# The third inner problem of a fast-product FFN makes its weight sums on VectorE; transposes and a plain weight tile move one or two products later

## The chip, the cores and the metric

The kernel runs on one NeuronCore of a Trainium2 chip. The metric is the device time of one execution, in microseconds (us). Three runs of the kernel before took 1898.81, 1896.77 and 1898.53 us, median 1898.53. TensorE is written PE here, VectorE DVE, ScalarE ACT, GpSimd POOL and SyncE SP, as the profile has them.

## The reference

Two layers, each a gated mixer of three branches and then a SwiGLU FFN, with a DeepNorm residual around both. x has 512 rows and 1024 columns, everything is float32. The change touches the FFN alone:

```python
u = jnp.einsum('bsd,df->bsf', x, w_ffn_in[l])
u_gate, u_up = jnp.split(u, 2, axis=-1)
ffn = jnp.einsum('bsf,fd->bsd', jax.nn.silu(u_gate) * u_up, w_ffn_out[l])
x = _layer_norm(DEEPNORM_ALPHA * x + ffn, ln2_g[l], ln2_b[l])
```

The hidden width is 2816 for the gate and for the up half each, that is 22 tiles of 128 columns.

## The kernel before

**Float32 by three products.** Each operand is carried as a high part and a low part. ACT casts the high part and DVE subtracts to get the low part (for weights: class `Staged`, lines 259 and 260, tiles `wh` and `wl`, read from a staging tile `st`). `mm3` (lines 122 to 124) then issues three matmuls for one product of tiles: high by high, high by low, low by high. Where activations are the stationary operand (`product`, output tile `pf`) the second of the three, line 123, already needs `wl`; where weights are stationary (`proj_T`, output `pt`) only the third does.

**Inner problems with seven products.** Columns 0 to 2047 of gate and up are made as four "inner problems" p, q, r, u (`u_fin(0..3, ...)`), of 512 gate and 512 up columns each. One splits into two by two blocks and is made with seven block products instead of eight (m1, m2, y, v, x, g, h). A product is one item: 2 row blocks of 4 times 3 matmuls of 128x512, 24 in all. Its weights are a quadrant of the matrix or a sum of quadrants; quadrant (i, j) means row half i, and gate (j = 0) or up (j = 1). Two classes make these sums:

- `Chain` keeps one staging tile `a` and adds quadrants to it by accumulating DMAs from POOL's queue (line 178): m1 uses (0,0); y uses (0,0)+(0,1), then v and m2 load fresh quadrants, and x and h use `a` after a second and a third accumulation. With the pair of transfers for g ("c") that is four loads on SP and four accumulations on POOL.
- `Close` loads `a` = (0,0)+(0,1) early (a load and one accumulation, "ahead_a"), loads (0,0) again for m1, (1,1) for v and (1,0) for m2, and lets DVE make the sums for x and h: `d += a` at v (line 233) and `e += d` at m2 (line 239). With "c" that is five loads on SP, two accumulations on POOL, and two additions of 128x2048 on DVE.

Before the change p and r are `Chain`, q and u are `Close`. The output product of the FFN has two problems of the same kind, o and w, both `Chain`; the six hidden tiles 16 to 21 are plain (`u_ffn(i)`, 48 matmuls each), the last two of them, 20 and 21, between products of o and w.

**What follows a product.** The gate half of a problem goes through tanh on ACT (line 1201), two DVE operations (1202 and, with the up half, 1210), and so into `nat`. `s_turn(pb, hf)` then transposes two such row tiles on PE (line 1222, eight 128x128 transposes, output `ph`), and ACT copies the two banks out (line 1224, `hf`). `s_ready`, `s_differ`, `s_sums` and `s_rest` make the operands of o and w from these.

**What sets the order.** A list of items, written out by hand (lines 1364 to 1377), gives the order of the products; the groups behind an item are pieces of work done between its row blocks. `run_items` fetches weights ahead until three weight tiles are in hand: three buffers for `wh` and `wl` rotate, so the split of an item's weights can begin when the item three before it has left PE. There are four staging tiles (`NSTAGE`), and a load can be issued on SP only when the tile's last reader is done. All loads stand in SP's queue in one order, the accumulations in POOL's. Each engine takes its instructions strictly in its own order, which a scheduler has fixed when the kernel is built: an instruction that waits holds up all that stands behind it.

Of the kernel before, what the change touches and what calls it, by code (L numbers as in the profile page):

```python
# [56 lines left out]
def trunk(ctx, tc, x_in, xT_in, w_in, ret_norm_g, da_norm_g, lq1, lk1, lq2, lk2, w_a, w_b, w_c, b_merge, w_out,  # L57
# [19 lines left out]
    def g(dt=F32, name="g"):  # L77
        return gp.tile([P, 512], dt, tag="g", name=name)
# [4 lines left out]
    def bank(name="ps"):  # L83
        return psp.tile([P, 512], F32, tag="ps", name=name)
# [256 lines left out]
    def proj_T(act, wt, c0, nk=KT, ps=None, half=None):  # L341

        ps = bank("pt") if ps is None else ps
        sl = slice(0, S) if half is None else slice(256 * half, 256 * half + 256)
        for k in range(nk):
            a = act[k]
            mm3(ps[:, sl], wt.hi[:, k, c0:c0 + P], wt.lo[:, k, c0:c0 + P], a.hi[:, sl], a.lo[:, sl],
                k == 0, k == nk - 1)
        return ps
# [188 lines left out]
    def item(specs, fn, *groups):  # L538

        items.append((specs, fn, groups))  # L540
# [62 lines left out]
    def layer(l):  # L603
# [7 lines left out]
        v = {}  # L611
# [116 lines left out]
        def u_two(hv, acts, left_done, right_done):  # L728

            t, onto = {}, {"x": "m1", "g": "m1", "h": "m1", "v": "y"}  # L730

            def it(name, use):
                def fn(wt):
                    for j in range(2):
                        t[name, j] = ps = product(acts, name, j, wt, t.pop((onto.get(name), j), None))
                        if name in ("x", "g"):
                            t["m1", j] = ps
                        use(j, ps)
                        between()
                return [getattr(hv, name)], fn  # L740

            def copy(to):
                def use(j, ps):
                    t[to, j] = g(name="t" + to)
                    nc.scalar.copy(t[to, j], ps)  # L745
                return use

            def m2(j, ps):
                c = t.pop(("c11", j))
                nc.vector.tensor_add(c, c, ps)  # L750
                left_done(j, c)

            def x(j, ps):
                c = t.pop(("c12", j))
                nc.vector.tensor_sub(c, c, ps)
                right_done(j, c)

            def gg(j, ps):
                c = t.pop(("c22", j))
                nc.vector.tensor_sub(c, c, ps)  # L760
                right_done(2 + j, c)

            def h(j, ps):
                left_done(2 + j, ps)

            use = {"m1": copy("c11"), "m2": m2, "y": copy("c22"), "v": copy("c12"), "x": x, "g": gg, "h": h}
            return {"c": hv.ahead_c, "a": getattr(hv, "ahead_a", None), **{k: it(k, fn) for k, fn in use.items()}}
# [87 lines left out]
        def v_away(dst, wd):  # L855


            def done(t, c):
                for hf in range(2):
                    s = g(F32R, "vhl")  # L860
                    s3 = s.rearrange("p (h x) -> p h x", x=2 * wd)
                    src = c[:, 256 * hf:256 * hf + 256].rearrange("p (h x) -> p h x", x=wd)
                    part_hi(s3[:, :, 0:wd], src)
                    part_lo(s3[:, :, wd:2 * wd], src, s3[:, :, 0:wd])
                    dst[t, hf] = dram.tile([P, 512], F32, name=f"v{l}_{wd}_{t}_{hf}")
                    nc.sync.dma_start(dst[t, hf], f(s))
            return done
# [237 lines left out]
        def u_rvg(hp):  # L1105
            return u_two(Close(W, 0, 4, (RV + 512 * hp, RG + 512 * hp)), xq,
                         functools.partial(rv_done, hp), functools.partial(rg_done, hp))

        w, p, q = u_two(Close(W, 0, 4, (CV, DV)), xq, v_away(cv, 64), v_away(dv, 128)), u_rvg(0), u_rvg(1)
# [73 lines left out]
        def ffn_spec(i):  # L1183
            w = w_ffn_in[l]
            return ([w[:, P * i:P * i + P], w[:, FFN + P * i:FFN + P * i + P]], KT)
# [4 lines left out]
        def ffn_done(i, pg, pu):  # L1190
            t = g(name="fth")
            nc.scalar.activation(t, pg, AF.Tanh, scale=0.5)
            nc.vector.scalar_tensor_tensor(t, t, 1.0, pg, op0=ALU.add, op1=ALU.mult)
            nc.vector.tensor_mul(t, t, pu)
            hid[i] = t
# [17 lines left out]
        def s_turn(pb, hf):  # L1213

            def fn():
                rows = [nat.pop((pb, 2 * hf + j)) for j in range(2)]
                for fp in range(2):
                    ps = bank("ph")
                    for i in range(2):
                        for j in range(2):  # L1220
                            o, c = 256 * i + P * j, P * (2 * fp + i)
                            nc.tensor.transpose(ps[:, o:o + P], rows[j][:, c:c + P], ident)
                    t = half[pb, hf, fp] = g(name="hf")
                    nc.scalar.activation(t, ps, AF.Copy, scale=0.5)
            return fn
# [3 lines left out]
        def s_ready(gi, fp):  # L1229
            def fn():  # L1230
                pa, pc, k = 2 * gi, 2 * gi + 1, 8 * gi + 2 * fp
                tw = twins[gi, fp] = Twins(half.pop((pa, 0, fp)), half.pop((pa, 1, fp)))
                tw.ready(half.pop((pc, 0, fp)))
                hid[k], hid[k + 1] = tw.each
            return fn

        def s_differ(gi, fp):
            def fn():
                twins[gi, fp].difference(half.pop((2 * gi + 1, 1, fp)))
            return fn  # L1240

        def s_sums(gi, fp):
            def fn():
                twins[gi, fp].sums()
            return fn

        def s_rest(gi, fp):
            def fn():
                twins.pop((gi, fp)).rest()
            return fn  # L1250
# [8 lines left out]
        def s_x1(k):  # L1259
            def fn():  # L1260
                if k == 0:
                    x1q.update({i: Quarters(x1T[i], x1T[i + 4]) for i in range(4)})
                x1q[k].sums(x1f.pop(k), x1f.pop(k + 4))
            return fn

        def s_natural(*ts):
            def fn():
                for t in ts:
                    x1["n"].natural(t)
            return fn  # L1270

        def u_fin(pb, kind):

            return u_two(kind(w_ffn_in[l], 0, 4, (512 * pb, FFN + 512 * pb)), x1q,
                         functools.partial(gate_half, pb), functools.partial(gated, pb))
# [13 lines left out]
        def u_ffn(i):  # L1289
            def fn(wt):  # L1290
                pg = proj_T(x1T, wt, 0)
                pu = proj_T(x1T, wt, P)
                ffn_done(i, pg, pu)
            return [ffn_spec(i)], fn
# [64 lines left out]

            return specs, (plain, chase)[hf]  # L1360

        p, q, r, u = u_fin(0, Chain), u_fin(1, Close), u_fin(2, Chain), u_fin(3, Close)
        o, w = fout_items(0), fout_items(1)
        for (specs, fn), *groups in [
            (u_ffn_first([16, 17]), [s_natural(0)], [s_x1(0)]), (p["m1"], [s_x1(1)], [s_x1(2)]),
            (u_ffn(18), [s_x1(3), s_natural(1)], [p["c"]]), (p["m2"], [s_natural(2)], [s_natural(3)]), (p["y"],),
            (p["v"], [q["a"]]), (u_ffn(19),), (p["x"],), (q["m1"],), (p["g"], [s_turn(0, 0)]), (q["y"],), (p["h"],),
            (q["v"], [q["c"]]), (q["m2"], [s_turn(0, 1)]), (q["x"],), (r["m1"],), (q["g"], [s_turn(1, 0)]), (r["m2"], [r["c"]]), (q["h"],),
            (r["y"], [u["a"]]), (r["v"], [s_turn(1, 1)]), (u["m1"],), (r["x"],), (u["y"], [s_ready(0, 0)]), (r["g"], [s_turn(2, 0)]),
            (u["v"], [s_ready(0, 1), u["c"]]), (r["h"],),  # L1370
            (u["m2"],), (o["m1"], [s_turn(2, 1)]), (u["x"], [s_differ(0, 0)], [s_differ(0, 1)]), (o["m2"],),
            (u["g"], [s_turn(3, 0)], [o["c"]]), (o["y"],), (u["h"], [s_sums(0, 0)], [s_sums(0, 1)]),
            (o["v"], [s_rest(0, 0)], [s_rest(0, 1)]), (u_ffn(20), [s_turn(3, 1)]), (o["x"], [s_ready(1, 0)], [s_ready(1, 1)]),
            (w["m1"], [s_differ(1, 0)]), (o["g"], [s_differ(1, 1)], [w["c"]]), (w["m2"], [s_sums(1, 0)]), (o["h"], [s_sums(1, 1)]),
            (w["y"], [s_rest(1, 0)]), (u_ffn(21), [s_rest(1, 1)], [s_hid(16, 17, 18)]), (w["v"], [s_hid(19, 20, 21)]), (w["x"],),
            (fout_rest(0),), (w["g"],), (w["h"],), (fout_rest(1),),
        ]:
            item(specs, fn, *groups)
# [59 lines left out]
```

## Time and profile before

| what | value |
|---|---|
| median of three runs | 1898.53 us |
| the profiled execution | 1898.61 us, of which the span from the first to the last instruction is 1896.8 us |
| PE busy, share of the span | 1870.7 us, 99% |
| DVE busy | 1344.4 us, 71% |
| ACT busy | 973.2 us, 51% |
| mean granted clock of PE | 0.997 |
| transfers | 297.69 MB, mean 157 GB/s |

The spans on PE, DVE and ACT overlap, so their times don't add. The profile's waits say for an idle stretch of an engine which instruction of which other engine ended it. The two FFN stretches that the change touches run from about 679 to 852 us (layer 0) and from about 1622 to 1796 us (layer 1).

### The profile page before, as it was taken

Reading aid. Unit: us, or ns where it says so; the run is one execution under the profiler, and the core shown is the slowest. Engines: PE = TensorE matmul, PEld = TensorE weight load, DVE = VectorE, ACT = ScalarE, POOL = GpSimd, SP = SyncE. Lnnn points to the kernel's source line nnn. Section 1 sums busy time; section 2 is a strip of 40 time slices with the busy share of each in tenths; the row PEclk is TensorE's granted clock in tenths of the full one; section 3 lists DMA queues with packets and bytes.
Section 4 is the critical chain, followed back from the end, with each engine's and each line's share of the span. In section 5 each row is a group of like instructions: output and inputs, shape, how many; then the busy total and the mean of one; then the engine's idle time right before and its main releaser. Section 6 shows DMA issues by size and latency. Waiting matters only on the chain. (4 is left out here: it accounts for less than half of the span.)

```text
span 1896.8 us, 23994 instructions
## 1 busy us (share of the span) xinstructions
PE 1870.7 (99%) x9138; PEld 1574.8 (83%) x9138; DVE 1344.4 (71%) x2055; ACT 973.2 (51%) x1579; POOL 124.5 (7%) x149
## 2 busy tenths in 40 slices
PE   9999999999999999999999999999999999999998
PEld 7888888888888888778898888888888888887786
DVE  6767756677665866788677768566776668766886
ACT  5545555566634455444355555455765344554441
POOL 2000000000001001000010000000000010011000
PEclk9999999999999999999999999999999999999999
DMA  9685443332155668687376844533322647687771
GB/s 280 168 277 146 122 165 106 119 123 67 60 194 135 179 162 215 193 198 195 124 196 173 279 111 144 168 105 95 122 78 73 208 98 199 171 207 200 179 198 45
DMA packets 220851, 297.69 MB, mean 157 GB/s; under 512 B 8516, under 2 KB 115104, under 8 KB 220736
## 3 DMA queue, kind: packets, MB, share of 16 engines
q1 hardware_dynamic: 192512, 241.20, 38.5%
q0 software_dynamic: 28224, 54.95, 16.8%
q8 instruction: 72, 1.18, 0.3%
q14 instruction: 43, 0.35, 0.1%
HBM read 273.00 MB, written 23.12 MB: 156 GB/s over the span
## 5 line engine op out<-in xcount | busy, mean ns | idle before, releaser
L122 PE MATMUL pt<-xTh,wh 128*128 128x512 f32 (+1 forms) x1072 | 397.6, 372 | 7.0 <-ACT wh L154 6.7
L260 DVE TENSOR_TENSOR wl<-st,wh 128x2048 fp32r<-128x2048 f32 x126 | 288.5, 2290 | 157.5 <-ACT wh L259 149.7
L123 PE MATMUL pt<-xTl,wh 128*128 128x512 f32 (+1 forms) x1072 | 394.0, 368 | 1.9 <-DVE xTl L112 1.9
L124 PE MATMUL pt<-xTh,wl 128*128 128x512 f32 (+1 forms) x1072 | 394.6, 369 | 1.1 <-DVE wl L155 1.1
L259 ACT CAST wh<-st 128x2048 fp32r<-128x2048 f32 x126 | 241.0, 1913 | 223.7 <-PE pf L124 109.3
L155 DVE TENSOR_TENSOR wl<-st,wh 128x1024 fp32r<-128x1024 f32 (+1 forms) x204 | 218.6, 1095 | 72.7 <-ACT wh L154 66.7
L154 ACT CAST wh<-st 128x1024 fp32r<-128x1024 f32 (+1 forms) x204 | 188.0, 948 | 151.5 <-issue 46.9
L122 PEld LDWEIGHTS pt<-xTh,wh 128*128 128x128 f32 x1072 | 202.3, 189 | 40.3 <-ACT wh L154 8.0
L124 PEld LDWEIGHTS pt<-xTh,wl 128*128 128x128 f32 x1072 | 202.4, 189 | 35.5 <-DVE wl L155 1.9
L123 PEld LDWEIGHTS pt<-xTl,wh 128*128 128x128 f32 x1072 | 202.7, 189 | 34.4 <-DVE xTl L112 2.3
L122 PE MATMUL pf<-wh,xTh 128*128 128x512 f32 x336 | 131.4, 391 | 1.1 <-ACT rph L106 0.8
L123 PE MATMUL pf<-wl,xTh 128*128 128x512 f32 x336 | 130.9, 390 | 0.0
L124 PE MATMUL pf<-wh,xTl 128*128 128x512 f32 x336 | 130.8, 389 | 0.0
L122 PE MATMUL pf<-wh,s43h 128*128 128x512 f32 x224 | 88.5, 395 | 0.0
L123 PE MATMUL pf<-wl,s12h 128*128 128x512 f32 x224 | 87.7, 392 | 0.0
L122 PE MATMUL pf<-wh,s12h 128*128 128x512 f32 x224 | 87.6, 391 | 0.0
L124 PE MATMUL pf<-wh,s12l 128*128 128x512 f32 x224 | 87.5, 392 | 0.0
L124 PE MATMUL pf<-wh,s43l 128*128 128x512 f32 x224 | 87.3, 390 | 0.0
L123 PE MATMUL pf<-wl,s43h 128*128 128x512 f32 x224 | 87.3, 390 | 0.0
L745 ACT COPY tc<-pf 128x512 f32<-128x512 f32 x84 | 48.2, 587 | 66.2 <-PE pf L124 64.7
L122 PEld LDWEIGHTS pf<-wh,xTh 128*128 128x128 f32 x336 | 63.1, 188 | 15.9 <-ACT rph L106 1.6
L124 PEld LDWEIGHTS pf<-wh,xTl 128*128 128x128 f32 x336 | 63.1, 188 | 13.1
(317 smaller groups left out, 3706.7 us busy)
## 6 DMA issues: line engine op xcount, KB each, us to landing
st<-in_w_in SPq DMA_DIRECT2D x60, 1024.0 KB, 5.4
st<-in_w_ffn_in SPq DMA_DIRECT2D x36, 1024.0 KB, 5.3
st<-in_w_ffn_in POOLq DMA_DIRECT2D x24, 1024.0 KB, 9.6
st<-in_w_ffn_out SPq DMA_DIRECT2D x20, 1024.0 KB, 6.4
st<-in_w_in SPq DMA_DIRECT2D x32, 512.0 KB, 5.2
st<-in_w_ffn_out POOLq DMA_DIRECT2D x16, 1024.0 KB, 9.5
st<-in_w_in POOLq DMA_DIRECT2D x12, 1024.0 KB, 11.4
th<-th SPq DMA_DIRECT2D x48, 256.0 KB, 4.9
```

The lines of the kernel that those rows point to most:

```text
L122: nc.tensor.matmul(ps, lh, rh, start=start, stop=False, skip_group_check=onto)
L123: nc.tensor.matmul(ps, lh, rl, start=False, stop=False, skip_group_check=onto)
L124: nc.tensor.matmul(ps, ll, rh, start=False, stop=stop, skip_group_check=onto)
L154: return [nc.scalar.copy(self.hi[:, a:b], self.st[:, a:b]), nc.vector.tensor_sub(self.lo[:, a:b], self.st[:, a:b], f(self.hi[:, a:b]))]
L155: nc.vector.tensor_sub(self.lo[:, a:b], self.st[:, a:b], f(self.hi[:, a:b]))]
L259: nc.scalar.copy(self.hi, st)
L260: nc.vector.tensor_sub(self.lo, st, f(self.hi))
L745: nc.scalar.copy(t[to, j], ps)
```

## The change

The third problem r becomes a `Close`, and the list of items is rewritten. The order of products from p's g on was

p.g, q.y, p.h, q.v, q.m2, q.x, r.m1, q.g, r.m2, q.h, r.y, r.v, u.m1, r.x, u.y, r.g, u.v, r.h, u.m2, o.m1, u.x, o.m2, u.g, o.y, u.h, o.v, tile 20, o.x

and is now

p.g, q.y, p.h, q.v, q.m2, q.x, r.m1, q.g, r.y, q.h, r.v, r.m2, r.x, u.m1, r.g, u.y, r.h, u.v, u.m2, u.x, o.m1, u.g, o.m2, u.h, o.y, tile 20, o.v, o.x.

The turning transposes stand one or two items later, and the plain tile 20 stands behind o.y instead of behind o.v.

```diff
-        p, q, r, u = u_fin(0, Chain), u_fin(1, Close), u_fin(2, Chain), u_fin(3, Close)
+        p, q, r, u = u_fin(0, Chain), u_fin(1, Close), u_fin(2, Close), u_fin(3, Close)
         o, w = fout_items(0), fout_items(1)
         for (specs, fn), *groups in [
             (u_ffn_first([16, 17]), [s_natural(0)], [s_x1(0)]), (p["m1"], [s_x1(1)], [s_x1(2)]),
             (u_ffn(18), [s_x1(3), s_natural(1)], [p["c"]]), (p["m2"], [s_natural(2)], [s_natural(3)]), (p["y"],),
-            (p["v"], [q["a"]]), (u_ffn(19),), (p["x"],), (q["m1"],), (p["g"], [s_turn(0, 0)]), (q["y"],), (p["h"],),
-            (q["v"], [q["c"]]), (q["m2"], [s_turn(0, 1)]), (q["x"],), (r["m1"],), (q["g"], [s_turn(1, 0)]), (r["m2"], [r["c"]]), (q["h"],),
-            (r["y"], [u["a"]]), (r["v"], [s_turn(1, 1)]), (u["m1"],), (r["x"],), (u["y"], [s_ready(0, 0)]), (r["g"], [s_turn(2, 0)]),
-            (u["v"], [s_ready(0, 1), u["c"]]), (r["h"],),
-            (u["m2"],), (o["m1"], [s_turn(2, 1)]), (u["x"], [s_differ(0, 0)], [s_differ(0, 1)]), (o["m2"],),
-            (u["g"], [s_turn(3, 0)], [o["c"]]), (o["y"],), (u["h"], [s_sums(0, 0)], [s_sums(0, 1)]),
-            (o["v"], [s_rest(0, 0)], [s_rest(0, 1)]), (u_ffn(20), [s_turn(3, 1)]), (o["x"], [s_ready(1, 0)], [s_ready(1, 1)]),
+            (p["v"], [q["a"]]), (u_ffn(19),), (p["x"],), (q["m1"],), (p["g"],), (q["y"], [s_turn(0, 0)]), (p["h"], [q["c"]]),
+            (q["v"], [r["a"]]), (q["m2"], [s_turn(0, 1)]), (q["x"],), (r["m1"],), (q["g"],), (r["y"], [s_turn(1, 0)]), (q["h"], [r["c"]]),
+            (r["v"], [u["a"]]), (r["m2"], [s_turn(1, 1)]), (r["x"],), (u["m1"],), (r["g"],), (u["y"], [s_turn(2, 0)]),
+            (r["h"], [u["c"]], [s_ready(0, 0)]), (u["v"], [s_ready(0, 1)]), (u["m2"], [s_turn(2, 1)]), (u["x"],),
+            (o["m1"], [s_differ(0, 0)], [s_differ(0, 1)]), (u["g"],), (o["m2"], [s_sums(0, 0)], [o["c"]]), (u["h"], [s_turn(3, 0)]),
+            (o["y"], [s_sums(0, 1)]), (u_ffn(20), [s_rest(0, 0)], [s_rest(0, 1)]), (o["v"], [s_turn(3, 1)]),
+            (o["x"], [s_ready(1, 0)], [s_ready(1, 1)]),
             (w["m1"], [s_differ(1, 0)]), (o["g"], [s_differ(1, 1)], [w["c"]]), (w["m2"], [s_sums(1, 0)]), (o["h"], [s_sums(1, 1)]),
```

**SP's queue where q goes over into r** (layer 0; a row is a load into a staging tile). Before, the five loads from q's "c" on: q.c (6239), r's chain tile (6256), r.m2 (6343), r.c (6445), r.v (6465).

```order
L174 DMA st_6239<-in_w_ffn_in 128x4x512
L174 DMA st_6256<-in_w_ffn_in 128x4x512
L174 DMA st_6343<-in_w_ffn_in 128x4x512
L174 DMA st_6445<-in_w_ffn_in 128x4x512
L174 DMA st_6465<-in_w_ffn_in 128x4x512
```

Now the eight loads from q's "c" on: q.c (6205), r's `a` (6242), r.m1 (6259), r.v (6409), r.m2 (6460), r.c (6483), u's `a` (6520), u.m1 (6537).

```order
L174 DMA st_6205<-in_w_ffn_in 128x4x512
L174 DMA st_6242<-in_w_ffn_in 128x4x512
L174 DMA st_6259<-in_w_ffn_in 128x4x512
L174 DMA st_6409<-in_w_ffn_in 128x4x512
L174 DMA st_6460<-in_w_ffn_in 128x4x512
L174 DMA st_6483<-in_w_ffn_in 128x4x512
L174 DMA st_6520<-in_w_ffn_in 128x4x512
L174 DMA st_6537<-in_w_ffn_in 128x4x512
```

The load 6256 used to serve r.m1; r.m1 now has a load of its own, 6259, in the staging tile that q.x's split leaves, directly behind the load of r's `a`, which is followed by an accumulation on POOL. The same pair stands again as 6520 and 6537 for u.

**DVE's order at the same place.** Before: q.x's split (6222), the gate of p, r.m1's split (6259), q.m2's sums and q.g's split (6312).

```order
L260 TENSOR_TENSOR wl_6222<-st_6145,wh_6221 128x2048
L1210 TENSOR_TENSOR fth_6217<-tc22_5937,fth_6217 128x512
L260 TENSOR_TENSOR wl_6259<-st_6256,wh_6258 128x2048
L750 TENSOR_TENSOR tc11_6084<-tc11_6084,pf_6263 128x512
L1202 TENSOR_SCALAR fth_6277<-fth_6277,tc11_6084 128x512
L750 TENSOR_TENSOR tc11_6099<-tc11_6099,pf_6294 128x512
L260 TENSOR_TENSOR wl_6312<-st_6239,wh_6311 128x2048
```

Now, with r.m1's split as 6262 and q.g's as 6314:

```order
L260 TENSOR_TENSOR wl_6225<-st_6131,wh_6224 128x2048
L1210 TENSOR_TENSOR fth_6220<-tc22_5937,fth_6220 128x512
L750 TENSOR_TENSOR tc11_6084<-tc11_6084,pf_6265 128x512
L1202 TENSOR_SCALAR fth_6279<-fth_6279,tc11_6084 128x512
L750 TENSOR_TENSOR tc11_6099<-tc11_6099,pf_6296 128x512
L260 TENSOR_TENSOR wl_6262<-st_6259,wh_6261 128x2048
L260 TENSOR_TENSOR wl_6314<-st_6205,wh_6313 128x2048
```

r.m1's split has moved behind q.m2's sums, directly ahead of q.g's split.

**ACT's order around the gate of r's last product, r.h** (tanh rows, line 1201, of 6809 and 6825). Before, the splits of o.m1 (6792), u.x (6829) and o.m2 (6869) stand ahead of it:

```order
L259 COPY wh_6792<-st_6790 128x2048
L259 COPY wh_6829<-st_6655 128x2048
L259 COPY wh_6869<-st_6867 128x2048
L745 COPY tc12_6788<-pf_6685 128x512
L1201 ACTIVATE fth_6809<-pf_6349 128x512
L1201 ACTIVATE fth_6825<-pf_6364 128x512
```

Now (6757 and 6776) the split of u.m2 (6740) stands ahead, and those of u.x (6788) and o.m1 (6830) behind:

```order
L259 COPY wh_6740<-st_6738 128x2048
L1201 ACTIVATE fth_6757<-pf_6349 128x512
L1201 ACTIVATE fth_6776<-pf_6364 128x512
L106 COPY qm1h_6780<-hf_6158 128x512
L259 COPY wh_6788<-st_6687 128x2048
L106 COPY qm2h_6784<-hf_6436 128x512
L745 COPY tc12_6804<-pf_6694 128x512
L106 COPY qm1h_6806<-hf_6165 128x512
L259 COPY wh_6830<-st_6828 128x2048
```

The split of o.m2, which stood two rows ahead of the tanh rows, is now fourteen rows behind them.

## The prediction

> **What bounds the kernel now.** I read the page's busy times first, then PE's waits, then the two FFN stretches by windows.
>
> ```profile
> PE 1870.7 (99%) x9138; PEld 1574.8 (83%) x9138; DVE 1344.4 (71%) x2055; ACT 973.2 (51%) x1579; POOL 124.5 (7%) x149
> ```
>
> PE is the bound: only time in which PE idles, or runs at a lower granted clock, can be won without taking matmuls away, and the change takes none away. The waits of PE over the whole span:
>
> ```profile
> PE pt L122 <- ACT wh L154: 6.7, 3, 3.5
> PE ph L1222 <- DVE fth L1210: 4.5, 2, 2.4
> PE pt L124 <- DVE wl L155: 1.1, 2, 0.5
> ```
>
> The turning transposes (L1222) wait for the gate twice, and a plain tile (L154 is its split) waits for its weights. The busy times of the two stretches from p.g's start to w.m1's start, one per layer, and of windows around three of the waits (columns: length; PE, PEld, DVE, ACT, POOL busy with instruction counts; PE clock; DMA share; GB/s):
>
> ```profile
> 678.87:852.31 173.44, 167.31 (x762) 138.21 (x760) 123.65 (x117) 87.81 (x95) 15.42 (x12) 0.99 0.76 189
> 1622.04:1795.70 173.66, 167.93 (x762) 138.19 (x760) 123.67 (x117) 87.84 (x95) 15.42 (x12) 0.99 0.76 189
> 794.00:802.00 8.00, 5.90 (x31) 4.67 (x30) 7.22 (x8) 6.02 (x8) 0.00 (x0) 1.00 0.44 155
> 822.00:834.00 12.00, 7.96 (x28) 5.82 (x27) 8.48 (x13) 6.84 (x9) 0.00 (x0) 0.86 0.67 225
> 1737.00:1750.00 13.00, 10.60 (x45) 8.51 (x44) 11.34 (x14) 8.42 (x10) 1.30 (x1) 0.87 0.63 224
> ```
>
> What would a stretch take undisturbed? Three starts of PE give the pace:
>
> ```profile
> 678.87 0.39 PE L122 MATMUL pf<-wh,s43h 128*128 128x512 f32 x1
> 685.20 0.39 PE L122 MATMUL pf<-wh,s12h 128*128 128x512 f32 x1
> 690.64 0.39 PE L122 MATMUL pf<-wh,xTh 128*128 128x512 f32 x1
> ```
>
> A product (q.y, from 685.20 to 690.64) takes 5.44 us; p.g with a turn inside takes 6.33, so a turn costs 0.89. The stretch holds 27 products, one plain tile of twice the matmuls and 8 turns: 27 x 5.44 + 10.88 + 8 x 0.89 = 164.9 us. Measured are 173.44 and 173.66: **8.5 and 8.8 us are lost, 17.3 in all**, 0.9% of the time. Idle is only part of it: in the window at 822 it is 4.04 us, and the clock of 0.86 over 12 us takes another 1.7; in the one at 1737 it is 2.40 and 1.7; in the one at 794 it is 2.10 with the clock at 1.00.
>
> **Why the transposes wait** (layer 0; ACT, DVE and PE by time, and the load that o.m2's split needed, with its time to landing):
>
> ```profile
> st<-in_w_ffn_out SPq DMA_DIRECT2D x1, 1024.0 KB, 7.0
> 783.40 2.29 DVE L260 TENSOR_TENSOR wl<-st,wh 128x2048 fp32r<-128x2048 f32 x1 [2.98 <-ACT wh L259]
> 792.84 1.91 ACT L259 CAST wh<-st 128x2048 fp32r<-128x2048 f32 x1 [9.47 <-DMA st<-in_w_ffn_out]
> 798.19 1.29 DVE L1210 TENSOR_TENSOR fth<-tc,fth 128x512 f32<-128x512 f32 x2
> 798.93 0.44 PE L1222 MATMUL ph<-ident,fth 128*128 128x128 f32 x2 [2.10 <-DVE fth L1210]
> ```
>
> u.x's split ended at 785.7 and freed the staging tile for o.m2's weights, which landed 7.0 us later. Until then ACT stood for 9.47 us at o.m2's split, and behind it in ACT's order the tanh of r.h, a product that PE had left three items earlier. The lateness is one of order, not of work.
>
> **Why the plain tile waits:**
>
> ```profile
> 812.49 2.29 DVE L260 TENSOR_TENSOR wl<-st,wh 128x2048 fp32r<-128x2048 f32 x1
> st<-in_w_ffn_in SPq DMA_DIRECT2D x2, 512.0 KB, 9.9
> 826.02 2.00 ACT L154 CAST wh<-st 128x1024 fp32r<-128x1024 f32 x2 [7.77 <-DMA st<-in_w_ffn_in]
> 827.12 0.50 PE L122 MATMUL pt<-xTh,wh 128*128 128x512 f32 x1 [3.51 <-ACT wh L154]
> ```
>
> Its staging tile came free when u.h was split, at 814.8; its two loads took 9.9 us by the median, and PE was there at 823.6.
>
> **The change part by part.**
>
> *Turn and gate of r.* Now only u.m2's split stands ahead of r.h's tanh on ACT, and o.m2's is fourteen rows behind. The turn falls inside u.m2, 8.2 us after r.h (u.v's 5.44 and half of u.m2). A sister in the same place relative to its Close problem exists in the trace, the turn inside q.m2:
>
> ```profile
> 701.68 0.68 DVE L1210 TENSOR_TENSOR fth<-tc,fth 128x512 f32<-128x512 f32 x1
> 704.25 1.03 PE L1222 MATMUL ph<-ident,fth 128*128 128x128 f32 x8
> ```
>
> Its gate is done 1.9 us ahead of PE. Around u.m2 one DVE piece of 0.68 is added and one split of 2.29 stands behind instead of ahead, so I take no wait there.
>
> *Plain tile.* Its weights now go into the tile that o.m2's split leaves. That split can start when u.x has left PE (three weight buffers), and the plain tile starts five products and one turn later, 5 x 5.44 + 0.89 = 28.1 us. Split (0.2 + 1.91 + 2.29), loads (9.9) and cast (1.04) need 15.5. The eight residual rows that o.m1 loads stand ahead in SP's queue as they did before. About 10 us are left: no wait.
>
> *r as Close.* Per layer it adds one load on SP and takes two accumulations from POOL; seven splits stay seven. On DVE two additions are new:
>
> ```profile
> L233 DVE TENSOR_TENSOR st<-st x10: 2283/2285/2294, 61.8 to 1706.8; 128x2048 f32<-128x2048 f32 x10
> ```
>
> 4 x 2.285 = 9.1 us for both layers. DVE is busy 123.65 of 173.44 us there, and behind the additions stand splits whose products are five and more microseconds off, so they cost nothing; without that cover they would cost the 9.1.
>
> *r.m1 and u.m1, the new risk.* r.m1 now needs its own load, into the tile that q.x's split leaves. The rows of that moment, where before the load for r.m2 went out:
>
> ```profile
> 699.48 2.28 DVE L260 TENSOR_TENSOR wl<-st,wh 128x2048 fp32r<-128x2048 f32 x1
> 701.79 0.37 SPq L174 DMA_DIRECT2D st<-in_w_ffn_in  x1
> 713.29 0.39 PE L122 MATMUL pf<-wh,xTh 128*128 128x512 f32 x1
> ```
>
> Nothing ahead of 701.79 moves, since it hangs on p.h, which starts at 690.64 in both orders. PE reaches r.m1 at 713.29, and its second matmul at 713.52 needs `wl`. Split and handovers take 0.1 + 1.91 + 0.05 + 2.29 = 4.35, so the load may take 713.52 - 701.79 - 4.35 = **7.4 us**. How long it takes depends on an accumulation that starts at the same time: that of r's `a`. Its load, and the load and accumulation of q's "c" ahead of it, stand in the trace (each issue with its time to landing behind it):
>
> ```profile
> 683.81 0.37 SPq L174 DMA_DIRECT2D st<-in_w_ffn_in  x1
> st<-in_w_ffn_in SPq DMA_DIRECT2D x1, 1024.0 KB, 5.1
> 689.43 1.28 POOL L178 DMA_DIRECT2D st<-in_w_ffn_in  x1 [28.02 <-DMA st<-in_w_ffn_in]
> st<-in_w_ffn_in POOLq DMA_DIRECT2D x1, 1024.0 KB, 9.9
> 691.99 0.37 SPq L174 DMA_DIRECT2D st<-in_w_ffn_in  x1
> st<-in_w_ffn_in SPq DMA_DIRECT2D x1, 1024.0 KB, 9.0
> ```
>
> The load of `a` landed at 701.0. POOL follows a landing by some 0.5 us (683.81 + 5.1 = 688.9 against 689.43). Now `a` goes out 0.9 us sooner (the turn no longer sits ahead of q.v's split) but shares with the same accumulation, so it lands at 700.4 to 701.0, and POOL issues at 701.0 to 701.6. r.m1's load goes out 0.2 to 0.8 us behind that. Nearest pairs, an SP load 0.37 ahead of an accumulation and one 0.83 behind:
>
> ```profile
> 1090.69 0.37 SPq L150 DMA_DIRECT2D st<-in_w_in  x1
> 1091.06 1.27 POOL L178 DMA_DIRECT2D st<-in_w_in  x1 [13.70 <-DVE wl L260]
> st<-in_w_in SPq DMA_DIRECT2D x1, 1024.0 KB, 5.5
> 133.92 1.28 POOL L178 DMA_DIRECT2D st<-in_w_in  x1 [29.84 <-DMA st<-in_w_in]
> 134.75 0.37 SPq L174 DMA_DIRECT2D st<-in_w_in  x1
> st<-in_w_in SPq DMA_DIRECT2D x1, 1024.0 KB, 9.5
> ```
>
> So the load takes between 5.5 (no wait) and 9.5 us (a wait of 2.1). On a line between the pairs, 0.2 to 0.8 gives 7.4 to 9.4, a wait of 0 to 2.0. u.m1 stands in the same relation to r as r.m1 to q, and both layers have both: four places. I take 1.2 us at each, 4.8 in all, a little over the middle because a wait leaves some slow matmuls behind it; ends 0 and 8.4.
>
> The half clock could come on top. In the trace an idle of 2.40 us drew a window of it and one of 2.10 did not, so waits up to 2 us are priced without it. The Trainium skill ("TensorE: Matmul & The Clock Gate", The HAM clock gate) says that the gate halves the clock after an idle window of about 3.4 us; by that no new wait of this size would draw it, and the sum would be the same, but the 2.40 in this trace did draw it, so here the trace decides and the half clock stays among the rivals.
>
> **Sum**, against the profiled execution, which took 1898.6 and is 0.1 above the median: 1898.6 - 17.3 + 4.8 = **1886.1 us**.
>
> **The rivals.**
>
> *No collision.* If the four loads land within 7.4 us, all 17.3 is kept: 1881.3. For it: the loads lie near the edge, and a slightly later `a` puts SP ahead, as in the 5.5 row. [...] Chance 0.22.
>
> *The transposes still wait.* If r.h's gate is late at u.m2 as it was before, only the plain tile's part is won: the turns' idle and clock (2.10 + 2.40 + 1.7 = 6.2) stays, and 1886.1 + 6.2 = 1892.3. Against it stands the sister without a wait. Chance 0.10.
>
> *Half clock at each new wait.* Two of the old stalls drew 1.7 us each. If all four new ones do: 1886.1 + 4 x 1.7 = 1892.9. Chance 0.08.
>
> *Slower: the four loads go wholly behind the accumulation.* The longest landing of a load beside accumulations in layer 0's FFN shows how far that can go (residual rows were in flight as well):
>
> ```profile
> st<-in_w_ffn_out SPq DMA_DIRECT2D x1, 1024.0 KB, 13.2
> ```
>
> A landing after 13.2 us makes a wait of 13.2 - 7.4 = 5.8 and surely the half clock, 7.5 each: 1898.6 - 17.3 + 30.0 = 1911.3. The change loses from 17.3 / 4 = 4.3 us per place on, that is a landing after 11.7 us, or after 10.0 if the half clock comes too. Against it: nothing but these two transfers is in flight there. Chance 0.10.
>
> **How the numbers follow.** The forecast of partial collisions has 0.50; its own range is 1881.3 to 1889.7 (0 to 8.4 lost). Taken with the rivals, 1880.5 to 1895 holds eight in ten: the two cases at 1892 lie inside, the slow one and half a microsecond of scatter below the best case outside. A change of under 0.2%, 3.8 us, can't be told from none here. Faster than 1894.8 are all cases but the slow one, and a little of the half-clock case is over the line: 0.87. Within 0.2% I give 0.04, slower 0.09, the slow rival cut a little.
>
> **What would show it.** In the profile after: PE's waits for the gate (L1222 on L1210) and for the plain tile (L154 at the second of the two in the stretch) gone; the two stretches from p.g to w.m1 at 165 to 169 us; new waits of PE on the `wl` of L260 at r.m1 and u.m1, four in all, about 1 us each; the SP loads ahead of them landing 5.5 to 9.5 us after issue, within a microsecond of an accumulation. Wrong would be: waits of over 4 us at these places, half-clock windows behind them, a turn that waits inside u.m2 or q.y, or an FFN stretch that is not shorter.

## The result, and the profile after

The changed kernel takes 1883.03 us, the median of four runs (1881.89, 1883.28, 1882.86, 1883.19); the kernel before takes 1898.67 us beside it. The ratio is **0.9918, 95% interval 0.9901 to 0.9935**: 15.6 us less. The profiled execution took 1881.89 us, its span is 1880.1 us, 16.7 us shorter than the span before.

The page's busy times:

```profile
PE 1865.1 (99%) x9138; PEld 1572.9 (84%) x9138; DVE 1353.0 (72%) x2059; ACT 974.2 (52%) x1579; POOL 119.2 (6%) x145
```

The same 9138 matmuls, 5.6 us less of PE's busy time. Some 3.4 of it is time at half clock which is gone (two windows of 3.41 us in the kernel before, half of each lost; a matmul counts as busy for longer there); the other 2 are not traced to single rows. The rest of the gain is idle time. PE's waits over the whole span now are these (us in total, times, longest):

```profile
PE pt L123 <- DVE xTl L112: 1.9, 2, 1.0
PE pt L122 <- ACT wh L154: 1.6, 1, 1.6
PE warm L574 <- POOL ident masks.py:199: 1.5, 1, 1.5
PE pf L122 <- ACT rph L106: 0.8, 2, 0.4
```

The waits for the gate (L1222 on L1210, 4.5 us before) are gone. What is left on L154 is one wait at the kernel's first weights, in the first ten microseconds. None of the four lies in the two FFN stretches; those for `xTl` stand in the FFN's first product, at 603.6 and 1538.4, and were there before. The two stretches from p.g's start to w.m1's, by windows (length; PE, PEld, DVE, ACT, POOL busy; PE clock; DMA share; GB/s):

```profile
678.95:843.86 164.91, 164.91 (x761) 137.25 (x760) 127.97 (x119) 88.38 (x95) 12.85 (x10) 1.00 0.74 191
1613.75:1778.66 164.91, 164.91 (x762) 137.25 (x760) 127.97 (x119) 88.39 (x95) 12.82 (x10) 1.00 0.74 191
```

Each takes 164.91 us, all of it busy and at full clock. They were 173.44 and 173.66, so 8.53 + 8.75 = 17.28 us came from here, and the other parts of the span gave back 0.6. DVE is busier by 4.3 us in each, about the two additions of r (2.29 us each).

**The four loads that the prediction feared** went like this; here the one with the least room, u.m1 in layer 1, with the accumulation beside it (start, length, engine):

```profile
1676.00 1.28 POOL L178 DMA_DIRECT2D st<-in_w_ffn_in  x1 [10.66 <-DMA st<-in_w_ffn_in]
1676.54 0.37 SPq L174 DMA_DIRECT2D st<-in_w_ffn_in  x1
```

Their times to landing in the view of transfers:

```profile
st<-in_w_ffn_in POOLq DMA_DIRECT2D x1, 1024.0 KB, 11.5
st<-in_w_ffn_in SPq DMA_DIRECT2D x1, 1024.0 KB, 6.0
```

The load goes out 0.54 us behind the accumulation and still lands in 6.0 us; the accumulation takes 11.5. The other three loads landed in 5.7, 5.7 and 5.9 us, where 7.4 were allowed. So at r.m1 in layer 0 (by time: the split on ACT and DVE, then PE's arrival):

```profile
707.68 1.91 ACT L259 CAST wh<-st 128x2048 fp32r<-128x2048 f32 x1 [0.82 <-DMA st<-in_w_ffn_in]
709.62 2.29 DVE L260 TENSOR_TENSOR wl<-st,wh 128x2048 fp32r<-128x2048 f32 x1 [0.80 <-ACT wh L259]
713.38 0.39 PE L122 MATMUL pf<-wh,xTh 128*128 128x512 f32 x1
713.61 0.39 PE L123 MATMUL pf<-wl,xTh 128*128 128x512 f32 x1
```

`wl` is ready at 711.91 and needed at 713.61: 1.7 us to spare. The turn inside u.m2 and the plain tile, each with the last operation that it waits for and PE's arrival:

```profile
779.90 0.68 DVE L1210 TENSOR_TENSOR fth<-tc,fth 128x512 f32<-128x512 f32 x1
784.07 0.71 PE L1222 MATMUL ph<-ident,fth 128*128 128x128 f32 x5
813.46 1.22 DVE L155 TENSOR_TENSOR wl<-st,wh 128x1024 fp32r<-128x1024 f32 x1
821.21 0.39 PE L122 MATMUL pt<-xTh,wh 128*128 128x512 f32 x1
```

The gate is done 3.5 us ahead of PE, the low part of the plain tile's weights 6.5 us, their cast (done at 811.68) 9.5 us.

### The profile page after: what moved, and what is told of

It is laid out like the page before. It is cut to its first block, busy times and chain, and to the rows that moved or that the text cites. A ratio compares the mean times of both kernels' runs of the same rounds, so it can differ in the third digit from the quotient of the medians.

```text
span 1880.1 us, 23994 instructions
## 1 busy us (share of the span) xinstructions
PE 1865.1 (99%) x9138; PEld 1572.9 (84%) x9138; DVE 1353.0 (72%) x2059; ACT 974.2 (52%) x1579; POOL 119.2 (6%) x145
## 5 line engine op out<-in xcount | busy, mean ns | idle before, releaser
L154 ACT CAST wh<-st 128x1024 fp32r<-128x1024 f32 (+1 forms) x204 | 188.0, 948 | 139.6 <-issue 55.2
L124 PEld LDWEIGHTS pf<-wh,xTl 128*128 128x128 f32 x336 | 63.1, 188 | 13.2
## 6 DMA issues: line engine op xcount, KB each, us to landing
st<-in_w_ffn_in POOLq DMA_DIRECT2D x20, 1024.0 KB, 10.4
```

The source lines that it names most:

```text
L124: nc.tensor.matmul(ps, ll, rh, start=False, stop=stop, skip_group_check=onto)
L154: return [nc.scalar.copy(self.hi[:, a:b], self.st[:, a:b]), nc.vector.tensor_sub(self.lo[:, a:b], self.st[:, a:b], f(self.hi[:, a:b]))]
```

## The experiments

Twelve kernels ran, each beside the kernel before on the same chip. Four questions: is it the order or the Close that gains; are the two old stalls independent, as the sum of the prediction has them; what makes a load beside an accumulation late; and how much room the additions have.

### Order or Close

`e1_chain`, the new order with the old kind of r:

```diff
-        ... u_fin(2, Close), u_fin(3, Close)
+        ... u_fin(2, Chain), u_fin(3, Close)
-            (q["v"], [r["a"]]),
+            (q["v"],),
```

> The changed order with r left a Chain (its sums by accumulating DMAs, no early load of r's `a`). If the new order alone brings the gain and Close is only a neighbour that costs nothing, the time is that of the changed kernel, 1883.0 within 2 us, and PE has no wait in the two FFN stretches. If Close is needed, because a Chain has only two products between r.m1 and r.y for an accumulation of 11 to 12 us and the split behind it (4.35 us), PE waits for r.y's weights by 1 to 5 us in each layer, with or without the half clock: 1885 to 1896.

`e2_close`, the old order with the new kind; r's own products stand in the order that Close needs (y, v, m2), so the run changes both at once:

```diff
-        ... u_fin(2, Chain), u_fin(3, Close)
+        ... u_fin(2, Close), u_fin(3, Close)
-            (q["v"], [q["c"]]), ... (r["m2"], [r["c"]]), (q["h"],), (r["y"], [u["a"]]), (r["v"], [s_turn(1, 1)]),
+            (q["v"], [q["c"], r["a"]]), ... (r["y"], [r["c"]]), (q["h"],), (r["v"], [u["a"]]), (r["m2"], [s_turn(1, 1)]),
```

> The kernel before with r as Close and r's own products in the order that Close needs (y, v, m2 for m2, y, v); everything behind r.m2, the turns and the plain tile stand where they stood. If the order of the later items makes the gain, the waits of PE for the gate (4.5 us) and for the plain tile (5.7 us and what follows it) stay: 1898.7 within 3 us. If taking accumulations off POOL's queue is what brings the loads in earlier, these waits shrink and the time falls below 1892.

| | order before | order after |
|---|---|---|
| r is a Chain | 1898.67 (the kernel before) | e1_chain 1883.89, ratio 0.9919 [0.9902, 0.9935] |
| r is a Close | e2_close 1907.13, ratio 1.0045 [1.0030, 1.0060] | 1883.03 (the changed kernel), 0.9918 [0.9901, 0.9935] |

The two new rows were run beside other executions of the kernel before (median 1898.29), from which their ratios come. The order brings the gain; Close brings nothing that these runs can tell in the new order, and together with its order of r's products it costs 8.8 us in the old one. The waits of PE in e1_chain that the changed kernel does not have:

```profile
PE pf L122 <- DVE tc L755: 2.1, 1, 2.1
PE pf L123 <- DVE wl L260: 0.5, 1, 0.5
```

They are in layer 0 alone, 2.6 us. In e2_close the extra wait is at u.y, and the rows show why (layer 0, by time):

```profile
743.68 0.37 SPq L174 DMA_DIRECT2D st<-in_w_ffn_in  x1
749.74 1.30 POOL L178 DMA_DIRECT2D st<-in_w_ffn_in  x1 [26.64 <-DMA st<-in_w_ffn_in]
758.41 1.91 ACT L259 CAST wh<-st 128x2048 fp32r<-128x2048 f32 x1 [5.57 <-DMA st<-in_w_ffn_in]
762.70 0.50 PE L123 MATMUL pf<-wl,s12h 128*128 128x512 f32 x1 [1.83 <-DVE wl L260]
```

u's `a` is loaded only at 743.68, when a staging tile comes free, and its accumulation lands at 758.3; the split of u.y is then 1.83 us late, in both layers. These waits are 3.7 of the 8.8 us, and a window at half clock behind the one in layer 1 takes some 1.7; the rest is not traced. In the changed kernel the same load went out some 11 us sooner against r.m1's start (at 731.05, with r.m1 at 713.38 instead of 714.90). All the old waits stayed as well: the gate's 5.2 us, the plain tile's 1.7 and 3.4.

`e8_late` asks which part of the order it is. It keeps the kernel before up to r.h and takes the changed rows from u.m2 on:

```diff
-            (u["m2"],), (o["m1"], [s_turn(2, 1)]), (u["x"], [s_differ(0, 0)], [s_differ(0, 1)]), (o["m2"],),
-            (u["g"], [s_turn(3, 0)], [o["c"]]), (o["y"],), (u["h"], [s_sums(0, 0)], [s_sums(0, 1)]),
-            (o["v"], [s_rest(0, 0)], [s_rest(0, 1)]), (u_ffn(20), [s_turn(3, 1)]), (o["x"], ...),
+            (u["m2"], [s_turn(2, 1)]), (u["x"],),
+            (o["m1"], [s_differ(0, 0)], [s_differ(0, 1)]), (u["g"],), (o["m2"], [s_sums(0, 0)], [o["c"]]), (u["h"], [s_turn(3, 0)]),
+            (o["y"], [s_sums(0, 1)]), (u_ffn(20), [s_rest(0, 0)], [s_rest(0, 1)]), (o["v"], [s_turn(3, 1)]),
+            (o["x"], ...),
```

> The kernel before (r a Chain, its order kept up to u.v and r.h) with the changed order from u.m2 on alone: the turn in u.m2, u.x ahead of o.m1, u.g ahead of o.m2, u.h ahead of o.y, the plain tile ahead of o.v. If this late part carries the gain, the waits for the gate and for the plain tile both go and the time is 1883 to 1886. If the earlier part (r's products and turns one place later) is needed too, because work of ACT and DVE that was late from there on is what makes the later stalls, PE still waits here for a gate or an operand by 2 to 3 us in each layer: 1888 to 1898.

1884.38 us (four runs, 1882.98 to 1885.09), ratio 0.9924 [0.9907, 0.9940]. The late part carries the gain. One wait is left in each stretch, the turn inside u.m2:

```profile
PE ph L1222 <- DVE fth L1210: 1.8, 2, 0.9
```

That is what the earlier half of the new order still removes.

### Are the two old stalls independent?

`e3_plain` and `e4_om2` each undo one stall of the kernel before, `e12_both` takes the two edits together.

```diff
-            (o["v"], [s_rest(0, 0)], [s_rest(0, 1)]), (u_ffn(20), [s_turn(3, 1)]),
+            (u_ffn(20), [s_rest(0, 0)], [s_rest(0, 1)]), (o["v"], [s_turn(3, 1)]),
```

> The kernel before with one edit: the plain tile 20 stands ahead of o.v, so that its two loads take the staging tile that u.g's split leaves. If the two stalls are independent, as the sum of the prediction has them, the plain tile's waits (3.51 + 0.53 us and 1.7 us of half clock in layer 0; 2.17 + 0.53 + 0.48 + 0.15 us in layer 1) go and the turns' stay: 1898.7 - 9.1 = 1889.6, down to 1887.6 with the 2 us of the stretches that no single wait explains. If one stall follows from the other, the time is either close to 1883 (this edit heals both) or stays above 1895.

```diff
-            ... (o["m2"],),
-            (u["g"], [s_turn(3, 0)], [o["c"]]), (o["y"],),
+            ... (u["g"], [s_turn(3, 0)]),
+            (o["m2"], [o["c"]]), (o["y"],),
```

> The kernel before with one edit: o.m2 stands behind u.g and not ahead of it, so that the split which is ahead of r.h's tanh in ACT's order is u.g's, whose weights are staged long before, and not o.m2's, whose load lands late. The turn stays where it was. If ACT's stand at o.m2's split makes the turn late, PE's wait for the gate goes: 1898.7 - 6.2 = 1892.5, and the plain tile's waits stay. If the turn waits because of its own place in the list, the time stays at 1898.7. If the plain tile's stall follows from ACT's stand (rival of independence), the time falls further, to 1883 to 1886.

> The kernel before with the edits of e3_plain and of e4_om2 together: the plain tile ahead of o.v, o.m2 behind u.g. If the two stalls of the kernel before only hide each other, both gone gives 1883 to 1886. If what each edit ran into (operands of w.m1 late by 3.0 us, operands of o.v late by 1.4 and 2.7 us) is work on ACT and DVE that stands too late in the old order, it is still there with both: 1888 to 1898.

| edit of the kernel before | us, median | ratio, 95% interval |
|---|---|---|
| e3_plain, plain tile ahead of o.v | 1899.81 (ten runs, 1897.30 to 1903.83) | 1.0007 [0.9998, 1.0017] |
| e4_om2, o.m2 behind u.g | 1896.39 (ten runs, 1892.36 to 1898.97) | 0.9988 [0.9978, 0.9997] |
| e12_both | 1885.94 (four runs, 1885.52 to 1885.99) | 0.9935 [0.9920, 0.9950] |

The stalls are not independent. Forecast were 9.1 and 6.2 us for the single edits; measured are about nothing and 2 us, and 12 for both. In e3_plain PE's wait for the plain tile's cast falls from 3.51 us to nothing in layer 0 and from 2.17 to 0.53 in layer 1, the gate's waits stay (4.8 us), and a new wait of 3.0 us appears at w.m1 in both layers, each with a window at half clock behind it (layer 0; DVE's rows by time, and PE's):

```profile
848.92 2.28 DVE L260 TENSOR_TENSOR wl<-st,wh 128x2048 fp32r<-128x2048 f32 x1
851.12 0.68 DVE L1303 TENSOR_TENSOR z<-z,pf 128x512 f32<-128x512 f32 x1
851.72 0.68 DVE L112 TENSOR_TENSOR qm1l<-hf,qm1h 128x512 fp32r<-128x512 f32 x1
852.46 0.79 PE L124 MATMUL pf<-wh,qm1l 128*128 128x512 f32 x1 [2.99 <-DVE qm1l L112]
```

PE comes to w.m1 sooner, and the low part of its operand stands behind a 2.28 us split in DVE's fixed order. In the profiled execution of e4_om2 (1893.79 us, one of the faster of the ten) the gate's two waits for `fth` are gone, and one of 0.7 and 0.6 us for the next problem's gate has come. The plain tile's two loads go out only some 2 us sooner against p.g's start than before, and now hold up another product (ACT's rows, then PE's):

```profile
821.17 1.05 ACT L154 CAST wh<-st 128x1024 fp32r<-128x1024 f32 x1 [5.58 <-DMA st<-in_w_ffn_in]
824.07 0.62 ACT L106 CAST qvh<-hf 128x512 fp32r<-128x512 f32 x1
824.74 0.50 PE L122 MATMUL pf<-wh,qvh 128*128 128x512 f32 x1 [1.44 <-ACT qvh L106]
```

ACT stands 5.58 us for the plain tile's weights, and the cast of o.v's operand is queued behind. The time that one edit frees is waited away at the next place; only when the places are clear together does PE run through. With both edits the largest wait left in the stretches is 0.7 us (layer 1):

```profile
PE ph L1222 <- DVE tc L1210: 1.0, 2, 0.7
PE pf L122 <- DVE tc L755: 0.8, 2, 0.6
```

### The loads beside an accumulation

`e5_late1` delays the loads of r.m1 and u.m1, by a DVE piece that is made twice ahead of the subtraction that frees their staging tile; `e6_late3` has three such pieces.

```diff
-            nc.vector.tensor_sub(self.lo, st, f(self.hi))
+            for n in [1] * again + [nk]: nc.vector.tensor_sub(self.lo[:, :n], st[:, :n], f(self.hi[:, :n]))
```

> The changed kernel with one extra DVE piece (0.69 us, a quarter of the subtraction made twice) ahead of the subtraction of q.x and of r.x, the two that free the staging tiles for the loads of r.m1 and u.m1; one gate operation (0.68 us) now also stands ahead of it, so the four loads go out some 1.4 us later, 1.1 to 1.9 us behind the accumulation beside them instead of -0.3 to +0.5. The load may then take 6.0 us. If a load that goes out over 0.8 us behind an accumulation takes 9 to 10 us, as the prediction has it, PE waits about 3.5 us at each of the four places, with the half clock up to 5.2: 1897 to 1904 us, and the profile shows landings of 9 to 10 us. If the accumulation never slows the load, the landings stay at 5.7 to 6.0 us and the time at 1883.

> The same with three extra pieces: the four loads go out some 2.8 us later and may take 4.6 us. Behind an accumulation at 9 to 10 us: a wait of 4.4 to 5.4 us at each place and the half clock behind it, 1902 to 1911 us. With landings of 5.7 to 6.0 us: a wait of 1.1 to 1.4 us at each place (up to 1.4 more where the subtraction of r.m1 now stands behind two more gate operations), 1887 to 1894 us.

e5_late1 took 1902.26 us, with ten runs from 1893.49 to 1906.83 (ratio 1.0016 [1.0000, 1.0032]); e6_late3 1906.56 us (1.0041 [1.0025, 1.0057]). In e5_late1 the loads go out 1.2 to 1.4 us later against p.g's start. The accumulations moved too, by 0.4 to 1.2 us, so that the loads stand 0.41 to 1.21 us behind them. In its profile, of an execution of 1895.07 us and so one of the faster, both u.m1 were late and both r.m1 were not. u.m1 in layer 0:

```profile
741.84 1.30 POOL L178 DMA_DIRECT2D st<-in_w_ffn_in  x1 [11.42 <-DMA st<-in_w_ffn_in]
742.61 0.37 SPq L174 DMA_DIRECT2D st<-in_w_ffn_in  x1
```

```profile
st<-in_w_ffn_in POOLq DMA_DIRECT2D x1, 1024.0 KB, 12.5
st<-in_w_ffn_in SPq DMA_DIRECT2D x1, 1024.0 KB, 9.4
```

0.78 us behind the accumulation, a landing after 9.4 us. PE's waits at the two places, 6.7 us, with two windows of 6.83 us at half clock behind them:

```profile
PE pf L123 <- DVE wl L260: 3.6, 2, 1.8
PE pf L122 <- ACT wh L259: 3.1, 2, 2.1
```

PE is busy for 11.85 of the two windows' 13.66 us, and half of that is lost: 6.7 + 5.9 = 12.6 us, and the profiled run is 13.2 above the changed kernel's. In e6_late3 all four loads were late, with landings of 8.4 to 10.4 us. `e9_noacc` has the same delay and no accumulation beside the loads:

```diff
-            self.more(self.a, 0, 1)
+            if self.cols[0] < 1024 or self.cols[1] - self.cols[0] < FFN: self.more(self.a, 0, 1)
```

> e5_late1 (the four loads some 1.4 us later) without the accumulation into r's and u's `a`: quadrant (0,1) is left out of these sums, two transfers per layer less. If the accumulation beside the load is what made it late, the four landings come down to 5 to 6 us, PE's waits at u.m1 go, and the time is 1882 to 1885 against e5_late1's 1902. If the later issue by itself was the cause, whatever is beside it, the waits of 1.0 to 2.1 and 1.8 us stay and the time stays above 1893.

1881.82 us (four runs, 1881.29 to 1883.51; 0.9916 [0.9901, 0.9930]), with no wait of PE in the stretches. Its load for u.m1 goes out as late against p.g's start as in e5_late1 and lands at its own pace:

```profile
742.19 0.37 SPq L174 DMA_DIRECT2D st<-in_w_ffn_in  x1
```

```profile
st<-in_w_ffn_in SPq DMA_DIRECT2D x1, 1024.0 KB, 5.1
```

So the accumulation makes the load late, not the late issue. The pair of `e10_touch_late` and `e11_touch` was meant to hold the accumulation back by a POOL operation on the weights that free the tile:

```diff
+            if self.late: nc.gpsimd.tensor_tensor(touched, f(blocks[-1].lo[:, 0, :1]), mhalf[:, :1], op=ALU.add)
             b = self.block(self.load(0, 0))
+            if self.late: self.more(self.a, 0, 1)
```

> e5_late1 with its four loads as late as there, but with the accumulations of r and u made to wait too: a POOL operation of 128x1 that reads the weights whose split frees the staging tile stands ahead of each. The accumulation then goes out at or behind the load, never 0.8 us ahead of it. If the order of the two issues decides, the landings are 5.5 to 6.1 us, which is as long as they may take there (6.0), so the waits at u.m1 go or stay under 0.5 us, and the time is 1883 to 1886. If the two transfers share the engines whoever goes first, the landings stay at 9 to 10 us and the time at 1893 to 1906.

> The changed kernel with the same four POOL operations and no delay. The loads go ahead of the accumulations at all four places: 1883.0 if the accumulation, which then lands up to 1 us later, still has its cover (r.y and u.y come two products behind). If it has none, PE waits for the split of r.y or u.y by up to 1 us at each place: up to 1888.

They failed as a test: nothing ties the two POOL operations together, and the profile shows the accumulation at 701.49 and the new operation at 702.95, behind it. e10_touch_late is then another late version, 1904.98 us (1.0044 [1.0028, 1.0061]), and e11_touch another changed kernel, 1882.55 us (0.9920 [0.9906, 0.9935]). Whether an accumulation that is held back makes the kernel safe was not tried.

All pairs of such a load and its accumulation in seven profiles (the changed kernel, e2_close at r.m1, e5_late1, e6_late3, e7_adds, e10_touch_late, e11_touch), by how far the load's issue lies behind the accumulation's:

| load behind the accumulation, us | pairs | load's time to landing, us | accumulation's first packet behind its issue, us |
|---|---|---|---|
| -0.60 to 0.54 | 14 | 5.59 to 6.11 | 3.7 to 5.4 |
| 0.76 and 0.78 | 2 | 8.25 and 9.38 | 4.2 and 4.1 |
| 1.13 to 2.78 | 10 | 8.44 to 11.27 | 2.0 |

Up to 0.54 us behind, a load takes little longer than e9_noacc's (5.1 to 5.4 us); from 1.13 us on it is late. In the two pairs between, the load's packets go first, but the accumulation comes in while over half of them are still to go (see the last section). The table holds for this place, where nothing else is in flight: in the kernel before, the load at 803.08 stood 0.25 us behind an accumulation and took 13.2 us, with residual rows moving as well.

### How much room the additions have

`e7_adds` doubles DVE's new work of r, another 9.1 us:

```diff
             b = self.block(self.d)
+            if self.cols == (1024, FFN + 1024): nc.vector.tensor_sub(b.lo, self.d, f(b.hi))
             nc.vector.tensor_add(self.d, self.d, self.__dict__.pop("a"))
```

(and the same at `self.e`).

> The changed kernel with DVE's two new additions of r each joined by another operation of the same size (the subtraction made twice, 2.29 us at r.v and at r.m2, both layers: 9.1 us more on DVE). If DVE's added work is hidden with room to spare, as the prediction has it, the time stays at 1883.0. If it is hidden only just, waits of PE for splits or gates behind r.v and r.m2 appear and the time rises by up to 9.1 us and the half clock on top, 1884 to 1899.

1895.22 us (ten runs, 1891.24 to 1897.69; 0.9984 [0.9975, 0.9993]), 12 us over the changed kernel. No gate and no split of r's products is waited for; all new waits are at u.m1 in both layers:

```profile
PE pf L122 <- ACT wh L259: 3.9, 2, 2.7
PE pf L123 <- DVE wl L260: 3.2, 2, 1.6
```

The extra operation moves the subtraction that frees u.m1's staging tile. The load goes out at 745.06, the accumulation at 742.95 (2.11 us before it), and it lands after 10.1 us. The work itself was hidden; what it pushed was not.

## Why the prediction was right, and where it was not

*17.3 us lost in the two stretches.* Right: 17.28 came back, and a stretch takes 164.91 us against the 164.9 worked out from three rows.

*The turn and the plain tile don't wait.* Right, with 3.5 us of room at the turn (1.9 at the sister that was taken for it) and 9.5 at the plain tile's cast, where the forecast counted about 10. Its own terms give 28.1 - 15.5 = 12.6; what takes the other 2.6 is not priced there.

*The additions are hidden.* Right for the change as it is. The reason given, that splits stand five and more microseconds ahead of their products, was too narrow: e7_adds shows that the next 9.1 us cost 12, through a load's issue and not through a split.

*Four loads at 1.2 us each, 4.8 us.* This term failed: it measured 0. The prediction put the loads 0.2 to 0.8 us behind the accumulations and read the wait from a straight line between the pairs at -0.37 and +0.83 us. In layer 0 they came at -0.08 and -0.26, since the load of r's `a` took 10.2 us and not 9, which put its accumulation at 701.95 instead of 701.0 to 701.6. In layer 1 they came at +0.32 and +0.54, inside the forecast, and landed in 5.9 and 6.0 us all the same: the straight line gave 7.8 and 8.5 there. Up to 0.54 us a load takes 6 us, from 0.76 on 8 to 11. So the rival "no collision" came true (1881.3; the profiled run has 1881.89), in layer 0 by the reason that it gave, a slightly later `a`, and in layer 1 because a load so little behind is not slowed. The case that had a chance of 0.50, partial collisions, did not happen. That the time still lies in its range, 1881.3 to 1889.7, is owed to a range that began at no loss.

*The slower rival* was real and near. A delay of 1.2 to 1.4 us made two of the four loads late in the profiled execution and put the time at 1893 to 1907, about the kernel before. In the changed kernel the closest load stood 0.22 us from the first late pair; its four runs lie within 1.4 us of each other, which leaves no room for a late load, worth 6.6 us in e5_late1's profile.

*What the right total hid.* The sum took the turn's 6.2 us and the plain tile's 11.1 as separate terms, and the rival "the transposes still wait" was priced from that, at 1892.3. e3_plain, e4_om2 and e12_both show that the terms don't add: alone 0 and 2 us, together 12. The total held because the change clears both places and all that lies between. Reading the stretch as a whole (27 products, a tile and 8 turns) was sound; dividing its loss among the waits that the profile names was not.

*Close* was costed at nothing by its operations. That holds in the new order (e1_chain) and fails in the old (e2_close), where u's `a` gets its staging tile some 11 us later. The part of the cost that the rows show is in when a staging tile is free, not in the operations.

The change did more than was needed: the late part of the order gives 1884.4 by itself, with r a Chain throughout.

## What to carry to other kernels

On a bound engine, price a stretch against its undisturbed length, and don't book the waits inside it as separate gains: one that is removed can come back at the next operand unless that is clear too. Before calling extra work on an idle engine free, look for the transfers whose start hangs on that engine's place in its order, and what else is in flight at that moment. Where a load and an accumulation start within a microsecond of each other, take an early and a late landing as possible and price each, rather than the mean.

## What the runs showed of the hardware that was not expected

**Who starts first goes first.** An accumulation's first packet came 2.0 us behind its issue where nothing was in its way, and in the 16 pairs in which the load went first the load's came 1.03 to 1.05 us behind its own. So the load's packets are first when it is issued less than some 0.96 us behind the accumulation (an estimate from these two times; no pair of the table lies between 0.78 and 1.13). Whichever comes second is then held off. In the changed kernel the accumulation of 1676.00 moved nothing until the load of 1676.54 was nearly through. Packets by queue (q1 is SP's, q0 POOL's) from 1677.3 to 1681.0, and from 1682.6 to 1687.5, when the load was done:

```profile
q1 hardware_dynamic: 414, 0.85, 83.9%
q0 software_dynamic: 442, 0.87, 97.2%
```

Its first packet came 5.4 us behind its issue, when 465 of the load's 512 packets had started. In e5_late1, with 0.78 us between the issues, the load was alone from 742.6 to 745.8 too, but the accumulation came in at 4.1 us, when 221 packets of the load had started; from 746.5 to 750.0 both moved side by side:

```profile
q0 software_dynamic: 207, 0.42, 68.9%
q1 hardware_dynamic: 202, 0.40, 36.3%
```

In e10_touch_late the accumulation of 747.31 was first, and the load of 748.44 waited 2.4 us for its first packet; from 749.3 to 750.8 q0 moved 68 packets and q1 none.

The Trainium skill ("DMA: Bandwidth & Descriptors", Queues, rings and completion order) has each engine take turns between its queues packet by packet. The rows of e5_late1 from 746.5 on agree with that; that the second queue moves nothing for some microseconds first does not follow from it, unless its packets were not ready before, which the trace does not show. What ends the holding off was not tested.

**Half the clock after half a window.** The windows at half clock start on a grid of 3.413 us within each execution: in the kernel before at 828.35 and 1743.12, which is 268.0 such steps apart. Whether a wait draws one depends on how much of one grid window it fills. The kernel before, grid windows around its waits of 2.40 and of 2.17 us in layer 1 (the clock is the third number from the end):

```profile
1739.71:1743.12 3.41, 1.01 (x6) 0.59 (x5) 3.41 (x6) 2.82 (x3) 0.00 (x0) 1.00 0.32 86
1743.12:1746.53 3.41, 3.41 (x12) 2.95 (x12) 3.23 (x3) 0.95 (x1) 0.00 (x0) 0.50 1.03 383
1767.02:1770.43 3.41, 1.71 (x8) 1.09 (x6) 0.00 (x0) 0.62 (x1) 0.00 (x0) 1.00 0.95 325
1770.43:1773.84 3.41, 2.41 (x9) 1.72 (x10) 2.96 (x4) 3.41 (x5) 0.00 (x0) 1.00 0.03 11
```

The first falls into one window, which PE fills for 1.01 of 3.41 us, and the next window is at half clock. The second is cut by the grid, 1.71 us busy in the first of its windows, and nothing follows. Over the FFN stretches of all profiles, a window at full clock with 1.87 us of idle or more was followed by one at half clock each time (19 windows), one with 1.79 us or less never; between them 1.80 drew it, 1.81 and 1.85 did not. A window already at half clock needs less: six with 0.87 to 1.64 us of idle were followed by a second, those with 0.45 or less never. The prediction compared the lengths of the waits, 2.40 against 2.10; what counts is where a wait lies. The Trainium skill ("TensorE: Matmul & The Clock Gate", The HAM clock gate) has a free-running window of 3413 ns, and the grid agrees with it; that an idle window is needed for the half clock does not, since here little over half of one is enough.
